# Forms written by ScalarE's queue, and branch blocks rounded where they lie, in a hybrid attention and convolution layer on one Trainium2 core

## The chip, the cores and the metric

The kernel runs on one core of a Trainium2 chip. The metric is the device time of one execution in microseconds. Three runs of the kernel before took 1036.29, 1038.19 and 1043.42 us; the median is 1038.19.

## The reference

One decoder layer for a sequence of 256 tokens with 2048 channels, all in float32. Cut to what matters here:

```python
h = _rmsnorm(x, pre_norm_g)
proj = jnp.einsum('bsd,de->bse', h, w_in)          # ten parts, see the split
(q_a, c_kv, k_rope, z_mla, c_in, b_gate, c_gate, z_conv, g_mla, g_conv) = jnp.split(proj, cuts, axis=-1)
...
q  = einsum(_rmsnorm(q_a), w_q_b)                   # 16 heads, 128 + 64 rotary
kv = einsum(_rmsnorm(c_kv), w_kv_b)                 # k_nope and v of 16 heads
attn = _causal_mla_attention(q_nope, q_rope, k_nope, k_rope, v)
attn = attn.reshape(b, s, MLA_WIDTH) * jax.nn.silu(z_mla)
y_mla = jnp.einsum('bse,ed->bsd', attn, w_o_mla)

u = c_gate * c_in
conv = sum(conv_w[k] * u_pad[:, k:k + s] for k in range(CONV_K))
y_conv = jnp.einsum('bse,ed->bsd', b_gate * conv * jax.nn.silu(z_conv), w_o_conv)

merged = jax.nn.sigmoid(g_mla) * y_mla + jax.nn.sigmoid(g_conv) * y_conv
x = x + _rmsnorm(jnp.einsum('bsd,de->bse', merged, w_out), post_norm_g)
```

All weights together are read once from DRAM, in units of 128 x 2048 float32 (1 MB).

## The kernel before

**Products.** A float32 value is split in a rounded part and the rest. `split_act` (L264) does it: ScalarE (ACT) rounds to `hi` (L265), VectorE (DVE) subtracts to `lo` (L266). A weight unit is loaded by SP's queue into `raw`, of which there are three slots (`load_raw`, L152), split in halves into `whi` and `wlo`, and multiplied on TensorE (PE), twice as many matmuls with `whi` as with `wlo`.

**Heads.** The first part loops over 16 heads. Around the attention of each head (queries `qn`, `qr`, keys `kn`, scores `sc` and `sw`, softmax `p`, its transposed `pt`, values `o`) it computes four units of the convolution path, `channels(h, 0)` to `channels(h, 3)`, whose sums `cv` are read by ACT (L811, L815, L818, tiles cv_f, cv_w, cg) or DVE before PE may overwrite them. Values are multiplied by their gate (L745) into `at_f`, four heads to a block: these four blocks are the attention's branch blocks. When the fourth head of a group is done, POOL's queue writes the block to DRAM (`far_at`, L749, 512 KB). The convolution's output goes by transposes and POOL writes to `far_cv` in the same way.

**Forms.** The gates g_mla and g_conv are products of x with two large weights. They are done as four sets s0 to s3 of seven products (Q1, V5, V6, V7, V3, V4, Q2) in place of eight, each with a combination of weights (DVE adds, L1272) and one of seven combinations of x, the "forms". `make_forms` (L876) prepares these while the heads run, a step at a time: three steps in each of the heads 0 to 13. It works in four chunks. For each, SP brings a part of x into `x_area` (256 KB twice), ACT scales it (L893), and then each of seven steps makes one form: ACT rounds (L907), DVE takes the rest (L909, L911), into one of three slots `form`. One step later the form's 256 KB are written to DRAM (`far_form`, L914), by SP's queue. ACT can round into a slot only when the write of the form three before has landed. The whole forms are read back by SP (`form`, L937) shortly before their product.

**Sets and branch blocks.** After the heads, the products of a set alternate with branch block products. p[0] to p[3] are the attention's (y_mla, sums `sq` with `at_both`), v[0] to v[3] the convolution's. Each has four weight units, one for each block, of 24 matmuls of 128x512 each (16 with `whi`, 8 with `wlo`); a named product of a set has 24 as well. `turned_unit` (above L969) loads a block from DRAM into a `raw` slot (`turned_at`, L969) and splits it into `at_both`. What follows on what is written by hand in calls of `interleave`; loads are then sorted by when their slot comes free and when they are needed, and issued up to 8 places ahead. For the first set:

```python
interleave(s0, {
    "Q1": p[0][:2], "V5": at_u[2:3] + p[0][2:3] + at_u[3:] + p[0][3:],
    "V6": p[1][:1], "V7": p[1][1:2], "V3": p[1][2:3], "Q2": p[1][3:] + p[2][:1],
})
```

Each engine and each of its DMA issues goes in the order of its own instructions: an instruction that waits holds back all that stand behind it on that engine. `tc.keep_in_program_order` fixes a place; the other instructions are moved by a scheduler.

Of the kernel before, what the change touches and what calls it, by code (L numbers as in the profile page):

```python
# [11 lines left out]
F32 = mybir.dt.float32  # L12
# [6 lines left out]
P = 128  # L19
S = 256  # L20
NT = S // P
# [61 lines left out]
def tile_layer(ctx: ExitStack, tc: tile.TileContext, xw, w0, xb, x, pos, pvec, post_g, wc, wz, wcv, wkr, wqk, wqr, wv, cwr, wsq, xf, out):  # L83
# [583 lines left out]
    def finish_all(*steps):  # L667
        for g in steps:
            for _ in g:
                pass  # L670
# [51 lines left out]
    def turn(p):  # L722

        pt = temp("pt", (P, 2, 3 * P), F32R, 1)
        hi, lo = (pt[:, j : j + 1, :].rearrange("p o (k q) -> p (o k) q", k=3) for j in range(2))
        split_act(quarters(hi), quarters(lo), by_rows(p[:, :], 3), True)
        return pt

    def values(h, pt):
        vv = groups["v", h // HV]  # L730
        j = h % HV
        o = bank(f"o{h}", tag="o", bufs=1)
        vs = slice(j * DV, (j + 1) * DV)
        both = o[:, :].rearrange("p (i q) -> p i q", i=2)
        mm = matmul
        mm(both, vv[0][:, 0, vs], pt[:, :, :S], start=True, stop=False)
        yield
        mm(o[:, :S], vv[1][:, 0, vs], pt[:, 0, :S], start=False, stop=False)
        mm(o[:, P:S], vv[1][:, 1, vs], pt[:, 0, S:], start=False, stop=False)
        mm(both[:, :, P:], vv[0][:, 1, vs], pt[:, :, S:], start=False, stop=True)  # L740

        at = at_t[:, h // HV, :, :].rearrange("p t (i k x) -> p t i k x", i=4, k=HV)[:, :, :, j, :]
        f = temp("f")
        whole(f[:, :], o)
        nc.vector.tensor_tensor(at, f[:, :].rearrange("p (t i x) -> p t i x", t=NT, i=4), at, op=ALU.mult)  # L745
        if j == HV - 1:
            g = h // HV
            tc.keep_in_program_order(
                nc.gpsimd.dma_start(out=far_at[g][:, :], in_=at_f[:, 4 * g : 4 * g + 4, :].rearrange("p k s -> p (k s)"))  # L749
            )  # L750


    at_t = at_f[:, :, :].rearrange("p (v t k) s -> p v t (k s)", v=NV, t=NT)
    far_at, far_cv, far_m = (
        [dram.tile([P, NT * 512], F32, name=f"far_{n}{g}") for g in range(4)] for n in ("at", "cv", "m")
    )
    z_ps = {}

# [31 lines left out]
    def channels(h, i):  # L790

        if i == 0:
            cv_ps["now"] = [bank(f"cv{h}_{t}", tag="cv", bufs=2) for t in range(NT)]
        quarter(cv_ps["now"], take(u_head[h][i]), i)
        if h == H - 2 and i in (0, 2):
            u = u_first[i // 2]
            tc.keep_in_program_order(nc.sync.dma_start(out=early[u][:, :], in_=plan[u][0]))
        if i == 3:
            if h == H - 1:
                at_u[0][0]()  # L800
                ahead(u_first[0])
                for u in at_u[:2]:
                    u[1](True)
            channels_done(*divmod(h, 4))

    def channels_done(j, n):
# [69 lines left out]
    def make_forms():  # L876

        kq = 2
        area = early_pool.tile([P, 2, kq, S], F32, name="x_area")
        sums_2 = [early_pool.tile([P, kq, P], F32, name=f"form_sum{i}") for i in range(2)]  # L880
        for c in range(KH // kq):
            for i in range(2):
                tc.keep_in_program_order(
                    nc.sync.dma_start(
                        out=area[:, i], in_=xf[i][:, c * kq * S : (c + 1) * kq * S].rearrange("p (k s) -> p k s", k=kq)
                    )
                )
            yield
            yield
            for i in range(2):  # L890
                for k in range(kq):
                    x = area[:, i, k, :]
                    nc.scalar.activation(x, x, AF.Copy, scale=col("pre_g", KH * i + kq * c + k))  # L893
            x = area[:, :, :, :].rearrange("p i k s -> p (i k) s")
            nc.vector.tensor_tensor(x, x, r_x[:, :].unsqueeze(1).to_broadcast([P, 2 * kq, S]), op=ALU.mult)
            yield
            a11, a21 = area[:, 0, :, :P], area[:, 0, :, P:]
            a12, a22 = area[:, 1, :, :P], area[:, 1, :, P:]
            u, w = (f[:, :, :] for f in sums_2)

            def tt(o, a, b, op):
                nc.vector.tensor_tensor(o, a, b, op=op)

            def part(n, src, sign=1.0):
                f = early_pool.tile([P, kq, 2, P], F32R, name=f"form{n}_{c}", tag="form", bufs=3)
                hi, lo = f[:, :, 0, :], f[:, :, 1, :]
                nc.scalar.activation(hi, src, AF.Copy, scale=sign)  # L907
                if sign == 1.0:
                    nc.vector.tensor_tensor(lo, src, hi.bitcast(F32), op=ALU.subtract)  # L909
                else:  # L910
                    nc.vector.scalar_tensor_tensor(lo, src, sign, hi.bitcast(F32), op0=ALU.mult, op1=ALU.subtract)  # L911
                w = kq * 2 * P
                return lambda: tc.keep_in_program_order(
                    nc.sync.dma_start(  # L914
                        out=far_form[n][:, c * w : (c + 1) * w], in_=f[:, :, :, :].rearrange("p k j c -> p (k j c)").bitcast(F32)
                    )
                )

            todo = (
                ("11", a11, 1.0, None), ("22", a22, 1.0, None), ("12", a12, 1.0, (u, a22, a21, ALU.subtract)),  # L920
                ("5", u, 1.0, (w, u, a11, ALU.add)), ("6", w, -1.0, (u, a11, a21, ALU.subtract)),
                ("7", u, 1.0, (w, w, a12, ALU.subtract)), ("3", w, 1.0, None),
            )
            for n, src, sign, following in todo:
                go = part(n, src, sign)
                if following:
                    tt(*following)
                yield
                go()
        while True:  # L930
            yield
# [64 lines left out]
            return list.__getitem__(self, i)  # L996

    at_b, cv_b = (Late(n, lambda i, n=n: both_tile(n, i)) for n in ("at", "cv"))
    at_u = [u for a, b in ((0, 2), (2, 3), (3, 4)) for u in turned_unit(far_at[a:b], at_b, a)]
    cv_u = [u for a, b in ((0, 2), (2, 4)) for u in turned_unit(far_cv[a:b], cv_b, a)]  # L1000
    for h in range(H):
        v, at = divmod(h, HV)
# [89 lines left out]
            rest = score(h + 1, later=True)  # L1092
        finish_all(*steps[::-1])
        if h == H - 1:
            pt = turn(ps_by_head.pop(h))
        channels(h, 3)
        if ahead_by_one:
# [4 lines left out]
        while len(coming) > ahead_by_one and h < H - 1:  # L1102
            arrive()
        if h == H - 1:
            finish_all(values(h, pt))
        if at == 3:
            coming.append(channels_join(v, 1))
        if at == 1 and h < H - 3:
# [251 lines left out]
    def interleave(s, after):  # L1360
# [12 lines left out]
    m_load = [turned_unit(far_m[a:b], m_b, a, tag, nc.gpsimd) for a, b, tag in ((0, 2, "rc0"), (2, 3, "rc1"), (3, 4, "rb1"))]  # L1373

    interleave(s0, {
        "Q1": p[0][:2], "V5": at_u[2:3] + p[0][2:3] + at_u[3:] + p[0][3:],
        "V6": p[1][:1], "V7": p[1][1:2], "V3": p[1][2:3], "Q2": p[1][3:] + p[2][:1],
    })
    interleave(s1, {"Q1": p[2][1:2], "V5": p[2][2:3], "V6": p[2][3:], "V7": p[3][:1], "V3": p[3][1:2], "V4": p[3][2:3], "Q2": p[3][3:]})
    interleave(s2, {  # L1380
# [288 lines left out]
```

## Time and profile before

| | |
|---|---|
| runs | 1036.29, 1038.19, 1043.42 us, median 1038.19 |
| profiled execution | 1039.11 us, of which the core's span 1037.3 |
| mean granted TensorE clock | 0.996 |
| busy: PE, DVE, ACT, POOL | 1011.0, 806.2, 591.8, 171.8 us |
| moved by DMA | 268.14 MB, 258 GB/s over the span |
| heads | to about 600 us of the span; sets and branch blocks follow |

Times of the trace are in microseconds from the start of the span. A row of a timeline has its start and length, the engine, the line, the operation, out<-in by the names of the tiles without their numbers, and how many instructions were grouped. Brackets give the idle time before it and what ended it. The rows of the waits give engine and line, what was waited for, and in total, times and longest. SPq, POOLq and ACTq are DMA issues of those engines.

### The profile page before, as it was taken

The page shows a single profiled execution, that of the slowest core. Times are in us where ns is not written, and L with a number is a line of the kernel's source. Part 1 is how long each engine was busy: PE and PEld are TensorE (multiplying, and loading weights), DVE is VectorE, ACT ScalarE, POOL GpSimd, SP SyncE. Part 2 cuts the span into 40 slices and gives each one's busy share as a digit, 9 for nine tenths or more (in the row PEclk, how much of TensorE's full clock was granted, in tenths as well). Part 3 has the DMA queues.
Part 4 walks back from the last instruction along what each step waited for, and adds up shares of the span by engine and source line. Part 5 has one row for each costly group of instructions (what it writes and reads, how often), then busy time and mean ns, then how long its engine had stood idle before and what let it go on. Part 6 is the DMA issues. An engine that isn't in the chain of part 4 may idle for free.

```text
span 1037.3 us, 13027 instructions
## 1 busy us (share of the span) xinstructions
PE 1011.0 (97%) x4552; PEld 836.9 (81%) x4552; DVE 806.2 (78%) x1103; ACT 591.8 (57%) x854; POOL 171.8 (17%) x315
## 2 busy tenths in 40 slices
PE   9999999999999999999999996999999999999997
PEld 8887888887888878778888875888788888878886
DVE  7589778767887677867787696889889779987562
ACT  7676656655665455555655463655665665565451
POOL 4520411203311222212133120000000101012000
PEclk9999999999999999999999998999999999999999
DMA  8775878668776688766688889697589979648842
GB/s 341 287 262 213 264 254 273 225 191 300 251 277 219 203 291 267 245 220 222 236 289 323 315 292 357 237 365 202 178 307 299 339 279 288 235 151 293 301 170 81
DMA packets 56674, 268.14 MB, mean 258 GB/s; under 512 B 9024, under 2 KB 13760, under 8 KB 31520
## 3 DMA queue, kind: packets, MB, share of 16 engines
q1 hardware_dynamic: 43488, 225.89, 59.9%
q0 software_dynamic: 12832, 40.23, 14.3%
q10 hardware_dynamic: 288, 1.20, 0.3%
q8 instruction: 35, 0.57, 0.2%
q14 instruction: 31, 0.25, 0.1%
HBM read 238.99 MB, written 24.12 MB: 254 GB/s over the span
## 4 chain that ended last, share of the span: by engine, by line
PE 88%; DMA 7%; DVE 3%; ACT 1%; issue 1%; SPq 0%; DVEq 0%; ACTq 0%
PE cv L88 28%; PE sq L88 16%; PE sX L88 8%; PE out L88 8%; PE z L88 8%; DMA far_form<-form 4%; PE sZ L88 4%; PE qa L88 2%; PE sY L88 2%; PE ckv L88 2%; PE vv L88 2%; PE kn L88 2%; PE qn L88 2%; DMA raw<-wsq_dram 1%; DVE wlo L266 1%; DMA x_area<-xf_dram 1%
## 5 line engine op out<-in xcount | busy, mean ns | idle before, releaser
L265 ACT ACTIVATE whi<-raw 128x1024 fp32r<-128x1024 f32 (+1 forms) x302 | 305.3, 1027 | 234.6 <-PE cv L88 89.4
L266 DVE TENSOR_TENSOR wlo<-raw,whi 128x1024 fp32r<-128x1024 f32 (+1 forms) x300 | 352.4, 1189 | 108.9 <-ACT whi L265 81.8
L88 PE MATMUL cv<-whi,x_both 128*128 128x512 f32 x1024 | 321.0, 390 | 4.7 <-ACT cv_f L811 2.9
L88 PEld LDWEIGHTS cv<-whi,x_both 128*128 128x128 f32 x1024 | 192.2, 188 | 46.1 <-ACT cv_f L811 3.7
L88 PE MATMUL cv<-wlo,x_both 128*128 128x512 f32 x512 | 199.6, 390 | 0.9 <-DVE wlo L266 0.9
L88 PEld LDWEIGHTS cv<-wlo,x_both 128*128 128x128 f32 x512 | 96.1, 188 | 20.3 <-DVE wlo L266 1.2
L266 DVE TENSOR_TENSOR slo_V<-b,shi_V 128x1024 fp32r<-128x1024 f32 x60 | 71.8, 1222 | 18.7 <-PE sq L88 12.1
L265 ACT ACTIVATE shi_V<-b 128x1024 fp32r<-128x1024 f32 x60 | 61.5, 1053 | 39.8 <-PE sq L88 22.7
L88 PE MATMUL z<-whi,x_both 128*128 128x512 f32 x256 | 79.9, 389 | 0.0
L366 POOL DMA_DIRECT2D far<-via x64 | 35.2, 557 | 227.1 <-DVE via L358 224.7
L88 PE MATMUL sq<-whi,at_both 128*128 128x512 f32 x256 | 63.4, 402 | 5.6 <-ACT whi L265 5.6
L88 PEld LDWEIGHTS sq<-whi,at_both 128*128 128x128 f32 x256 | 49.9, 195 | 16.7 <-ACT whi L265 6.0
L88 PE MATMUL sq<-whi,cv_both 128*128 128x512 f32 x256 | 60.6, 389 | 0.0
L88 PEld LDWEIGHTS sq<-whi,cv_both 128*128 128x128 f32 x256 | 48.0, 188 | 10.0
L88 PEld LDWEIGHTS z<-whi,x_both 128*128 128x128 f32 x256 | 48.1, 188 | 9.9
L88 PE MATMUL z<-wlo,x_both 128*128 128x512 f32 x128 | 49.8, 389 | 0.0
L88 PE MATMUL out<-whi,m_both 128*128 128x512 f32 x208 | 49.4, 389 | 0.0
L88 PE MATMUL sX<-shi_V,form 128*128 128x512 f32 x192 | 47.4, 389 | 0.0
L88 PEld LDWEIGHTS out<-whi,m_both 128*128 128x128 f32 x208 | 39.0, 188 | 8.1
L88 PEld LDWEIGHTS sX<-shi_V,form 128*128 128x128 f32 x192 | 36.0, 188 | 7.5
L1263 POOL DMA_DIRECT2D b<-wsq_dram x8 | 6.9, 863 | 208.6 <-DVE b L1272 95.7
L265 ACT ACTIVATE shi_Q<-b 128x1024 fp32r<-128x1024 f32 x28 | 28.8, 1052 | 22.1 <-PE sq L88 17.7
(305 smaller groups left out, 1572.7 us busy)
## 6 DMA issues: line engine op xcount, KB each, us to landing
raw<-wcv_dram SPq DMA_DIRECT2D x64, 1024.0 KB, 6.3
raw<-wsq_dram SPq DMA_DIRECT2D x48, 1024.0 KB, 6.9
b<-wsq_dram SPq DMA_DIRECT2D x26, 1024.0 KB, 5.1
raw<-wz_dram SPq DMA_DIRECT2D x16, 1024.0 KB, 4.9
raw<-wqk_dram SPq DMA_DIRECT2D x8, 1024.0 KB, 7.6
b<-wsq_dram POOLq DMA_DIRECT2D x8, 1024.0 KB, 9.2
far_form<-form SPq DMA_DIRECT2D x28, 256.0 KB, 7.5
form<-far_form SPq DMA_DIRECT2D x7, 1024.0 KB, 10.9
```

Of the source, the lines that this page charges most:

```text
L88: return tc.keep_in_program_order(nc.tensor.matmul(*a, **kw))
L265: a = nc.scalar.activation(hi, src, AF.Copy)
L266: b = nc.vector.tensor_tensor(lo, src, hi.bitcast(F32), op=ALU.subtract)
L366: tc.keep_in_program_order(queue.dma_start(out=f[i], in_=m))
L1263: tc.keep_in_program_order(nc.gpsimd.dma_start(out=dst[:, :], in_=wsq[n, c + b, k], accum_op=ALU.add))
```

## The change

Three things, in the words of the code. First, `far_form` is written by ACT's queue (`nc.scalar`) and not by SP's; the bringing of the next part of x moves one step ahead, to the last form of a chunk, and the first gets a step of its own. Second, the branch blocks no longer go to DRAM and back: `split_branch` rounds block i from `at_f` where it lies. Block 2 is rounded in the last head's `channels(15, 3)`, 0 and 1 before that head's `turn`, and 3 after its values; the first unit of p[0] is loaded and split ahead of those. Third, all four units of p[0] follow Q1, ahead of V5, and the units of p[1] move up or down to fit.

```diff
--- before.py
+++ after.py
@@ -743,16 +743,11 @@
         f = temp("f")
         whole(f[:, :], o)
         nc.vector.tensor_tensor(at, f[:, :].rearrange("p (t i x) -> p t i x", t=NT, i=4), at, op=ALU.mult)
-        if j == HV - 1:
-            g = h // HV
-            tc.keep_in_program_order(
-                nc.gpsimd.dma_start(out=far_at[g][:, :], in_=at_f[:, 4 * g : 4 * g + 4, :].rearrange("p k s -> p (k s)"))
-            )
 
 
     at_t = at_f[:, :, :].rearrange("p (v t k) s -> p v t (k s)", v=NV, t=NT)
-    far_at, far_cv, far_m = (
-        [dram.tile([P, NT * 512], F32, name=f"far_{n}{g}") for g in range(4)] for n in ("at", "cv", "m")
+    far_cv, far_m = (
+        [dram.tile([P, NT * 512], F32, name=f"far_{n}{g}") for g in range(4)] for n in ("cv", "m")
     )
     z_ps = {}
 
@@ -797,10 +792,8 @@
             tc.keep_in_program_order(nc.sync.dma_start(out=early[u][:, :], in_=plan[u][0]))
         if i == 3:
             if h == H - 1:
-                at_u[0][0]()
                 ahead(u_first[0])
-                for u in at_u[:2]:
-                    u[1](True)
+                split_branch(2)
             channels_done(*divmod(h, 4))
 
     def channels_done(j, n):
@@ -878,13 +871,17 @@
         kq = 2
         area = early_pool.tile([P, 2, kq, S], F32, name="x_area")
         sums_2 = [early_pool.tile([P, kq, P], F32, name=f"form_sum{i}") for i in range(2)]
-        for c in range(KH // kq):
+        def bring(c):
             for i in range(2):
                 tc.keep_in_program_order(
                     nc.sync.dma_start(
                         out=area[:, i], in_=xf[i][:, c * kq * S : (c + 1) * kq * S].rearrange("p (k s) -> p k s", k=kq)
                     )
                 )
+
+        bring(0)
+        yield
+        for c in range(KH // kq):
             yield
             yield
             for i in range(2):
@@ -911,7 +908,7 @@
                     nc.vector.scalar_tensor_tensor(lo, src, sign, hi.bitcast(F32), op0=ALU.mult, op1=ALU.subtract)
                 w = kq * 2 * P
                 return lambda: tc.keep_in_program_order(
-                    nc.sync.dma_start(
+                    nc.scalar.dma_start(
                         out=far_form[n][:, c * w : (c + 1) * w], in_=f[:, :, :, :].rearrange("p k j c -> p (k j c)").bitcast(F32)
                     )
                 )
@@ -925,6 +922,8 @@
                 go = part(n, src, sign)
                 if following:
                     tt(*following)
+                if n == "3" and c < KH // kq - 1:
+                    bring(c + 1)
                 yield
                 go()
         while True:
@@ -996,7 +995,11 @@
             return list.__getitem__(self, i)
 
     at_b, cv_b = (Late(n, lambda i, n=n: both_tile(n, i)) for n in ("at", "cv"))
-    at_u = [u for a, b in ((0, 2), (2, 3), (3, 4)) for u in turned_unit(far_at[a:b], at_b, a)]
+
+    def split_branch(i):
+        for t in range(NT):
+            split_turned(at_t[:, i, t, :], at_b[i], t, True)
+
     cv_u = [u for a, b in ((0, 2), (2, 4)) for u in turned_unit(far_cv[a:b], cv_b, a)]
     for h in range(H):
         v, at = divmod(h, HV)
@@ -1092,6 +1095,8 @@
             rest = score(h + 1, later=True)
         finish_all(*steps[::-1])
         if h == H - 1:
+            split_branch(0)
+            split_branch(1)
             pt = turn(ps_by_head.pop(h))
         channels(h, 3)
         if ahead_by_one:
@@ -1102,7 +1107,11 @@
         while len(coming) > ahead_by_one and h < H - 1:
             arrive()
         if h == H - 1:
+            load_raw(done["raw"])
+            split_unit(done["split"])
+            done.update(raw=done["raw"] + 1, split=done["split"] + 1)
             finish_all(values(h, pt))
+            split_branch(3)
         if at == 3:
             coming.append(channels_join(v, 1))
         if at == 1 and h < H - 3:
@@ -1373,8 +1382,7 @@
     m_load = [turned_unit(far_m[a:b], m_b, a, tag, nc.gpsimd) for a, b, tag in ((0, 2, "rc0"), (2, 3, "rc1"), (3, 4, "rb1"))]
 
     interleave(s0, {
-        "Q1": p[0][:2], "V5": at_u[2:3] + p[0][2:3] + at_u[3:] + p[0][3:],
-        "V6": p[1][:1], "V7": p[1][1:2], "V3": p[1][2:3], "Q2": p[1][3:] + p[2][:1],
+        "Q1": p[0], "V5": p[1][:1], "V6": p[1][1:2], "V7": p[1][2:3], "Q2": p[1][3:] + p[2][:1],
     })
     interleave(s1, {"Q1": p[2][1:2], "V5": p[2][2:3], "V6": p[2][3:], "V7": p[3][:1], "V3": p[3][1:2], "V4": p[3][2:3], "Q2": p[3][3:]})
     interleave(s2, {
```

Where the instructions go, at two places. The first is ACT at the end of head 8's channels, at the forms of the third chunk: form7_2 and form3_2 are forms 7 and 3 of that chunk, form3_2 takes the slot of form5_2 and so waits for its write; cv8 are the sums of head 8's channels, raw and whi are numbered by weight unit, qr, half, sc and sw belong to the next head's queries and scores. Before:

```order
L265 ACTIVATE whi76_0_3798<-raw76_3730 128x1024
L433 ACTIVATE half_3715<-qr5_3688 128x256
L907 ACTIVATE form3_2_3913<-form_sum1_1015 128x2x128
L811 ACTIVATE cv_f_110<-cv8_0_3547,r_both_97 128x512
L265 ACTIVATE whi76_1024_3802<-raw76_3730 128x1024
L265 ACTIVATE qr_3709<-f_3714 64x256 x2
L811 ACTIVATE cv_f_110<-cv8_1_3548,r_both_97 128x512
L695 ACTIVATE sc_half_3767<-sc9_3701 128x128
```

In the changed kernel, from the same cv_f on:

```order
L804 ACTIVATE cv_f_110<-cv8_1_3539,r_both_97 128x512
L695 ACTIVATE sc_half_3756<-sc9_3690 128x128
L695 ACTIVATE half_3757<-sw9_3691 128x256
L265 ACTIVATE whi77_0_3827<-raw77_3785 128x1024
L265 ACTIVATE qr_3698<-f_3703 64x256 x2
L904 ACTIVATE form7_2_3902<-form_sum0_1010 128x2x128
L265 ACTIVATE whi77_1024_3831<-raw77_3785 128x1024
L265 ACTIVATE pt_3859<-p_3458 128x384
L911 DMA far_form5_650<-form5_2_3820 128x512
L265 ACTIVATE whi78_0_3869<-raw78_3825 128x1024
L904 ACTIVATE form3_2_4108<-form_sum1_1011 128x2x128
L265 ACTIVATE whi78_1024_3873<-raw78_3825 128x1024
```

form3_2 stood ahead of both cv_f and now stands behind them, and the write that it waits for stands two rows ahead of it on the same queue, one whi apart.

The second place is SP's queue at the start of the first set. raw115 to raw118 are the weights of the four units of p[0], raw119 those of p[1]'s first; first_rb and first_rc are weights of the set's products, form_5, form_6 and form_7 the forms of V5, V6 and V7, turned_at2 and turned_at3 the blocks 2 and 3. Before:

```order
L167 DMA raw116_5798<-wsq_dram 128x2048
L1258 DMA first_rb0_5783<-wsq_dram 128x2048
L1258 DMA first_rb1_5784<-wsq_dram 128x2048
L937 DMA form_5_5782<-far_form5_654 128x2048
L969 DMA turned_at2_5803<-far_at2_642 128x1024
L1258 DMA first_rc0_5787<-wsq_dram 128x2048
L1258 DMA first_rc1_5788<-wsq_dram 128x2048
L167 DMA raw117_5828<-wsq_dram 128x2048
L969 DMA turned_at3_5852<-far_at3_643 128x1024
L937 DMA form_6_5789<-far_form6_655 128x2048
L167 DMA raw118_5943<-wsq_dram 128x2048
L937 DMA form_7_5790<-far_form7_656 128x2048
```

In the changed kernel:

```order
L167 DMA raw116_5805<-wsq_dram 128x2048
L167 DMA raw117_5807<-wsq_dram 128x2048
L1267 DMA first_rb0_5792<-wsq_dram 128x2048
L1267 DMA first_rb1_5793<-wsq_dram 128x2048
L936 DMA form_5_5791<-far_form5_650 128x2048
L1267 DMA first_rc0_5796<-wsq_dram 128x2048
L1267 DMA first_rc1_5797<-wsq_dram 128x2048
L167 DMA raw118_5827<-wsq_dram 128x2048
L936 DMA form_6_5798<-far_form6_651 128x2048
L167 DMA raw119_5852<-wsq_dram 128x2048
```

Both turned_at are gone, raw117 stands ahead of the set's first weights, raw118 ahead of form_6, and raw119 right behind form_6.

## Prediction

> **What bounds the kernel now.** I read the page first, for the engines and the transfers.
>
> ```profile
> PE 1011.0 (97%) x4552; PEld 836.9 (81%) x4552; DVE 806.2 (78%) x1103; ACT 591.8 (57%) x854; POOL 171.8 (17%) x315
> ```
>
> PE is busy for 1011.0 of 1037.3 us, so 26.3 us of idle time, with whatever is lost to a low clock, is all that a change which leaves the products alone can win. The change adds and removes no matmul. The next question is where those 26.3 us lie. PE's timeline at the end of the heads, where the products sX and sZ of the first set and the products sq of the branch blocks alternate, answers for the larger half (start, length, what ran, then the idle time before it and what ended that):
>
> ```profile
> 605.88 3.79 PE L88 MATMUL sq<-whi,at_both 128*128 128x512 f32 x16
> 611.16 0.73 PE L88 MATMUL sq<-wlo,at_both 128*128 128x512 f32 x2 [1.49 <-DVE wlo L266]
> 612.30 1.66 PE L88 MATMUL sq<-wlo,at_both 128*128 128x512 f32 x6 [0.41 <-DVE wlo L266]
> 613.79 3.79 PE L88 MATMUL sq<-whi,at_both 128*128 128x512 f32 x16
> ...
> 619.23 1.98 PE L88 MATMUL sZ<-shi_V,form 128*128 128x512 f32 x8
> ...
> 638.67 6.51 PE L88 MATMUL sq<-whi,at_both 128*128 128x512 f32 x16 [5.61 <-ACT whi L265]
> ...
> 646.84 1.98 PE L88 MATMUL sX<-shi_V,form 128*128 128x512 f32 x8
> ```
>
> The sixteen first matmuls of a unit take 3.79 us at 605.88 and 6.51 at 638.67, after a pause of 5.61 us: 2.7 more. The windows say why (length, busy time of PE, PEld, DVE, ACT and POOL, granted clock, DMA share, GB/s):
>
> ```profile
> 620.00:640.00 20.00, 12.22 (x49) 9.08 (x48) 13.90 (x14) 7.58 (x11) 0.89 (x1) 0.94 1.03 321
> 640.00:645.00 5.00, 5.00 (x14) 3.88 (x14) 4.42 (x4) 3.21 (x4) 0.00 (x0) 0.57 1.01 428
> ```
>
> The granted clock is 0.57 from 640 to 645, and the DMA engines are full in both windows. [...] What the pause waited for stands in SP's queue, the chain that ended last, and ACT's timeline, a row or a few of each:
>
> ```profile
> 612.27 0.33 SPq L167 DMA_DIRECT2D raw<-wsq_dram  x1
> 616.62 0.33 SPq L969 DMA_DIRECT2D turned_at<-far_at  x1
> 621.94 0.33 SPq L937 DMA_DIRECT2D form<-far_form  x1
> ...
> 624.69 12.76 DMA raw<-wsq_dram
> ...
> 637.56 2.00 ACT L265 ACTIVATE whi<-raw 128x1024 fp32r<-128x1024 f32 x2 [12.01 <-DMA raw<-wsq_dram]
> ```
>
> The weights of the last p0 unit were asked for at 624.69 and landed 12.76 us later; ACT stood for 12.01 us. Ahead of that issue on the queue are turned_at, which also holds a weight slot, and a form.
>
> The other losses that the change can touch lie earlier. First a row of the waits, ACT's, in all and how many times, then PE's stalls beside the making of the forms:
>
> ```profile
> ACT form L907 <- DMA far_form<-form: 30.5, 13, 6.1
> ...
> 141.87 0.39 PE L88 MATMUL sc<-kn,qn_hi 128*128 128x256 f32 x1 [0.54 <-DVE kn L266]
> 249.24 0.50 PE L88 MATMUL cv<-whi,x_both 128*128 128x512 f32 x1 [0.80 <-ACT cv_f L811]
> 386.07 0.50 PE L88 MATMUL cv<-whi,x_both 128*128 128x512 f32 x1 [2.10 <-ACT cv_f L811]
> 416.75 0.39 PE L88 MATMUL sc<-kn,qn_hi 128*128 128x256 f32 x1 [2.45 <-DVE kn L266]
> 447.17 0.50 PE L88 MATMUL cv<-whi,x_both 128*128 128x512 f32 x1 [1.77 <-ACT cv_w L815]
> ```
>
> ACT stood 13 times, 30.5 us in all, until a form's slot had been written away. The five stalls of PE sum to 0.54 + 0.80 + 2.10 + 2.45 + 1.77 = 7.66 us.
>
> **Branch blocks and their order.** Four writes far_at, four reads turned_at and their two weight slots go: 8 x 512 KB, 4 MB. The roundings of the blocks stay as many as before, on ACT and on DVE; they stand earlier. From 605.88 to 646.84 PE runs four units p0 and the product V5. A unit or a product is 24 matmuls, undisturbed from 613.79 to 619.23, 5.44 us. So 5 x 5.44 = 27.2 us of work took 40.96: 13.8 us lost.
>
> ```profile
> 604.22 3.89 ACT L265 ACTIVATE whi<-raw 128x1024 fp32r<-128x1024 f32 x4
> ...
> 620.95 1.14 ACT L265 ACTIVATE at_both<-turned_at 128x512 fp32r<-128x512 f32 x2
> ```
>
> What comes in its place, by hand from these rows: two roundings of a block on ACT, 1.14 us by the pair at 620.95, now stand ahead of the conv gate (cg) and of the weights' rounding at 604.22, and cg waits for a product on DVE that is itself behind a rounding. I let whi begin 2 us later. It was just in time (PE went on at 605.88 without a gap), so the first unit waits 2.0 us, and the 1.90 us for wlo that it stood before fall inside that: it ends at 605.9 + 2.0 + 5.4 = 613.3. The last p0 unit's weights need only the slot that the first unit's rounding frees near 612. At the 12.76 us of before they land at 624.8 and are rounded at 625.9, 1.7 us late, as that unit begins at 613.3 + 2 x 5.44 = 624.2; at the median of such loads, 6.9 us (below), they are 4 us early. I take no wait. Four p0 units and V5 then end at 613.3 + 4 x 5.44 = 635.1, 11.7 us earlier.
>
> Late next is p1's first unit, due at 635.1. Its weights stand on SP behind the form of V6, and that waits until POOL's writes far_cv have landed:
>
> ```profile
> 609.29 0.71 DVE L358 STREAM_TRANSPOSE cw<-cv_f 128x512 f32<-128x512 f32 x1
> ...
> 610.29 2.20 POOL L366 DMA_DIRECT2D far_cv<-cw  x4 [2.12 <-DVE cw L358]
> ...
> 616.85 0.55 POOL L366 DMA_DIRECT2D far_cv<-mv  x1 [2.74 <-DMA far_at<-at_f]
> ```
>
> The transpose falls behind roundings on DVE, to about 614; eight issues of 0.55 us reach 618.5, and the last landing came 5.1 us after its issue (616.85 to SP's next issue at 621.94), so SP is free near 623.5. At 12.76 us the weights land at 636.8 and are rounded at 637.9: a new wait of about 3 us. Bounds: none at 6.9 us; 6 us if the landing takes 16, and then, as before after 5.61, the half clock with its 2.7. I take 3, as the DMA engines stay near full. Net of these parts: 11.7 - 3.0 = **8.7 us**, bounds 3.0 and 11.7.
>
> **Forms by ACT's queue.** In the new order a form's write stands just ahead of the form that waits for its slot, in the typical place one whi of 1.06 us apart, some 25 times in 28. The wait on ACT is then about L - 1.1, where L is the write's time to landing. Rows of the form tiles, of the DMA issues (KB each, median us to landing) and of two windows:
>
> ```profile
> L914 SPq DMA_DIRECT2D far_form<-form x28: 327/427/784, 109.0 to 520.4; - x28
> ...
> DMA to landing us min/median/max: 3.8/7.7/14.8
> ...
> raw<-wsq_dram SPq DMA_DIRECT2D x48, 1024.0 KB, 6.9
> ...
> p<-far POOLq DMA_DIRECT2D x16, 192.0 KB, 4.8
> ...
> far_at<-at_f POOLq DMA_DIRECT2D x4, 512.0 KB, 5.9
> ...
> gb<-post_g_dram ACTq DMA_DIRECT2D x1, 1024.0 KB, 4.9
> ...
> 942.00:948.00 6.00, 6.00 (x28) 4.99 (x27) 6.00 (x10) 2.21 (x3) 2.54 (x5) 1.00 0.82 288
> 80.00:525.00 445.00, 436.47 (x2021) 363.09 (x2020) 347.27 (x587) 253.50 (x418) 89.67 (x164) 1.00 0.73 246
> ```
>
> The issues themselves, 28 x 0.43 = 12 us, go to an engine that is 57% busy; its lead over PE (next rows) hides them, and without that lead each would cost 0.43. On SP's queue 256 KB took a median of 7.7 us, among loads of 1 MB on the same queue. No write on ACT's queue is shown. Its one large transfer, 1 MB, issued at 942.9, landed in 4.9 us at a DMA share of 0.82, above the 0.73 of the forms' stretch; POOL's 192 KB took 4.8 and its writes of 512 KB 5.9. I take L = 4.7, nearest to ACT's own row; the bounds are 3.8, SP's fastest, and 7.7.
>
> How long ACT can stand unnoticed is in the trace too:
>
> ```profile
> 248.19 0.42 ACT L907 ACTIVATE form<-form_sum 128x256 fp32r<-128x256 f32 x1 [4.78 <-DMA far_form<-form]
> ...
> 385.03 0.42 ACT L907 ACTIVATE form<-form_sum 128x256 fp32r<-128x256 f32 x1 [6.08 <-DMA far_form<-form]
> ...
> 413.40 1.71 ACT L893 ACTIVATE x_area<-x_area,pv 128x256 f32<-128x256 f32 x4 [3.26 <-DMA x_area<-xf_dram]
> ```
>
> The first two waits stood ahead of cv_f and cost PE the 0.80 and 2.10 above; 4.78 - 0.80 and 6.08 - 2.10 are both 3.98 us of cover. At L = 4.7 a wait is 3.6, below it, so 0.54, 0.80, 2.10 and 1.77 go, 5.2 us. The 2.45 is not a form's: ACT stood 3.26 us for x_area, ahead of kn, and that load keeps its place on SP between the same weights, with one write less ahead of it; I let 0.8 go. Some of the 25 waits have less cover than 4 us; for those I take back 1.0. Net: **5.0 us**, bounds 6.5 (all but 1.2 of the 7.66) and a loss of 15.6 (first rival).
>
> **Sum.** 8.7 + 5.0 = 13.7 us off the profiled execution's 1039.11 is 1025.4. That execution lies 0.9 above the median of the runs, 1038.19; I say 1025.
>
> **Rivals.**
>
> ACT waits for its own writes (slower): if L is SP's 7.7 us, each wait is 6.6, 2.6 beyond the cover. Of 13 waits before, four stand beside a stall (0.54, 0.80, 2.10, 1.77); the same share of 25 is 8, so 8 x 2.6 = 20.8 us of stalls come and 5.2 go: 15.6 lost against 8.7 won, 1046. It decides from L = 5.1, and the kernel is slower than before from about L = 6.8. [...] The trace speaks against it as far as one transfer can, with 4.9 us for four times the bytes. Chance 0.10.
>
> The pause moves to p1: the wait of 6 us with half clock costs 8.7 where I took 3, 1031. For it: the landing of 12.76 us and the 321 GB/s (6.4 MB in 20 us), of which turned_at and far_at were 1 MB. Against: 12.76 was itself taken in the fullest stretch. 0.15.
>
> Forms gain nothing, L being near POOL's 5.9 so that 8 x 0.65 = 5.2 us of new stalls replace the old: 1030. 0.13.
>
> The change doesn't do what it says at the set's start: DVE, the engine behind the 1.49 and 0.41, gets its roundings in a burst and every unit waits for wlo; the 8.7 come back and 3 to 4 from the forms stay, 1036. 0.07.
>
> All waits go, p1's and x_area's too: 13.8 + 7.7 - 2.0 = 19.5 won, 1019.6. It is the near end of my forecast.
>
> **How the numbers follow.** The forecast, 1019 to 1029, has 0.55. The slower rival lies outside the range 1017 to 1037, the others inside; with the tails it leaves out some 0.15. A difference of 1%, 10.4 us, is about what a measurement of this kernel can tell from no change. Below 1027.8 lie nearly all of the forecast and some of the second and third rivals: 0.62. Above 1048.6 lies only the first rival with L over 8: 0.05. The rest, 0.33, is within 1%.
>
> **What would show it.** Right: far_form landing in about 4.7 us on ACT's queue; no stall of PE beside cv_f near 249 and 386; four p0 units in a row with one first wait of about 2 us, and no 12 us wait of ACT for raw; some 3 us of waiting at p1's first unit. Wrong: waits of ACT for far_form that average above 5 us, or a second stretch at half clock after V5.

## The result, and the profile after

The changed kernel took 1027.85 us in the median of four runs (1023.01, 1025.78, 1029.92, 1030.71) against 1038.60 for the kernel before on the same chip: a ratio of 0.989, 95% interval 0.9864 to 0.9916. Run again as an experiment it took 1026.72, ratio 0.9887 (0.9854 to 0.9919). The forecast was 1025. The first profiled execution took 1023.01 us with a span of 1021.2; the sum of the prediction for it was 1025.4.

Page of the changed kernel: the engines, then a group of its DMA issues (KB each, median us to landing) and two rows of its waits (total, times, longest).

```profile
PE 1006.6 (99%) x4552; PEld 835.5 (82%) x4552; DVE 805.2 (79%) x1103; ACT 591.4 (58%) x854; POOL 170.8 (17%) x311
...
far_form<-form ACTq DMA_DIRECT2D x28, 256.0 KB, 5.0
...
ACT form L904 <- DMA far_form<-form: 40.9, 14, 5.9
...
ACT whi L265 <- DMA raw<-wsq_dram: 10.9, 6, 3.6
```

PE's idle time fell from 26.3 to 14.6 us. The writes of the forms land in 5.0 us where they took 7.5, but ACT waits longer for them in all, 40.9 us against 30.5. Its wait for the set's weights fell from 18.7 us, 12.0 at the longest, to 10.9 and 3.6.

PE's timeline: the longest pause left in the heads, then from the first product of the set on:

```profile
411.89 0.39 PE L88 MATMUL sc<-kn,qn_hi 128*128 128x256 f32 x1 [1.97 <-DVE kn L266]
...
593.47 2.01 PE L88 MATMUL sX<-whi,form 128*128 128x512 f32 x8
...
601.08 3.98 PE L88 MATMUL sq<-whi,at_both 128*128 128x512 f32 x16 [1.97 <-ACT whi L265]
604.90 1.98 PE L88 MATMUL sq<-wlo,at_both 128*128 128x512 f32 x8
606.71 3.79 PE L88 MATMUL sq<-whi,at_both 128*128 128x512 f32 x16
...
617.59 3.79 PE L88 MATMUL sq<-whi,at_both 128*128 128x512 f32 x16
...
623.03 1.98 PE L88 MATMUL sZ<-shi_V,form 128*128 128x512 f32 x8
...
628.47 3.79 PE L88 MATMUL sq<-whi,at_both 128*128 128x512 f32 x16
...
683.76 1.98 PE L88 MATMUL sX<-shi_Q,form 128*128 128x512 f32 x8
```

Four p0 units and V5 run in a row, behind one wait of 1.97 us. p1's first unit follows at 628.47 without any. From 600 to 650 us the granted clock stays full, where before it was 0.57 in one window:

```profile
600.00:650.00 50.00, 48.92 (x215) 40.39 (x216) 44.83 (x40) 30.56 (x34) 6.19 (x10) 1.00 0.82 282
```

Why p1 does not wait is in the queues, POOL's and SP's issues and ACT's rounding of p1's weights:

```profile
609.67 2.18 POOL L366 DMA_DIRECT2D far_cv<-mv  x4
...
604.78 0.33 SPq L167 DMA_DIRECT2D raw<-wsq_dram  x1
613.42 0.33 SPq L936 DMA_DIRECT2D form<-far_form  x1
613.85 0.85 SPq L167 DMA_DIRECT2D raw<-wsq_dram  x2
...
624.73 2.01 ACT L265 ACTIVATE whi<-raw 128x1024 fp32r<-128x1024 f32 x2 [3.15 <-DMA raw<-wsq_dram]
```

The last p0 unit's weights are asked for at 604.78, ahead of everything that waits. SP comes free at 613.42, 2.1 us after POOL's last write was issued (the four writes in the first row start 0.55 us apart), and p1's weights land by 624.7, 10.9 us after their issue: rounded before 626.8, at least 1.7 us early.

Two distances hold all that changed much: from the start of the span to Q1 of the first set (the heads), and from there to Q1 of the second set, both read from PE's timelines. What follows took 336.1 us before and 336.5 to 337.5 us in the executions below.

| kernel (profiled execution) | heads | first set |
|---|---|---|
| before | 600.40 | 100.84 |
| the change, first profile | 593.47 | 90.29 |
| the change, second profile | 599.03 | 90.96 |
| forms by ACT's queue alone | 595.90 | 100.14 |
| branch blocks and order alone | 602.59 | 90.61 |
| the change, old order of p[0] | 597.83 | 100.35 |
| change, x by POOL's queue | 590.64 | 90.40 |
| change, forms by SP, x by POOL's queue | 596.90 | 90.95 |

The set is about 10 us shorter wherever the branch blocks and the order are both changed, and not with the order of before. The heads vary by 5.6 us between two executions of one kernel.

### The profile page after: what moved, and what is told of

It reads as the page before. It is cut to its first block, busy times and chain, and to the rows that moved or that the text cites. A ratio compares the mean times of both kernels' runs of the same rounds, so it can differ in the third digit from the quotient of the medians.

```text
span 1021.2 us, 13014 instructions
## 1 busy us (share of the span) xinstructions
PE 1006.6 (99%) x4552; PEld 835.5 (82%) x4552; DVE 805.2 (79%) x1103; ACT 591.4 (58%) x854; POOL 170.8 (17%) x311
## 4 chain that ended last, share of the span: by engine, by line
PE 85%; DMA 6%; ACT 3%; DVE 3%; issue 1%; POOL 1%; SPq 0%; DVEq 0%; ACTq 0%; POOLq 0%
PE cv L88 28%; PE sq L88 16%; PE out L88 9%; PE sX L88 7%; PE z L88 6%; PE sZ L88 4%; PE qa L88 2%; PE sY L88 2%; DMA x_area<-xf_dram 2%; PE ckv L88 2%; PE kn L88 2%; PE qn L88 2%; PE vv L88 2%; DMA far<-cw 1%; DMA b<-wsq_dram 1%
## 5 line engine op out<-in xcount | busy, mean ns | idle before, releaser
L88 PEld LDWEIGHTS cv<-whi,x_both 128*128 128x128 f32 x1024 | 192.3, 188 | 40.9 <-ACT cv_w L808 1.5
L265 ACT ACTIVATE shi_V<-b 128x1024 fp32r<-128x1024 f32 x60 | 61.6, 1054 | 40.9 <-PE sq L88 23.8
L88 PE MATMUL sq<-whi,at_both 128*128 128x512 f32 x256 | 60.8, 390 | 2.0 <-ACT whi L265 2.0
L265 ACT ACTIVATE shi_Q<-b 128x1024 fp32r<-128x1024 f32 x28 | 28.8, 1053 | 21.7 <-PE sq L88 19.1
```

Of the source, the lines that this page charges most:

```text
L88: return tc.keep_in_program_order(nc.tensor.matmul(*a, **kw))
L265: a = nc.scalar.activation(hi, src, AF.Copy)
```

## The experiments

**The change again.** Unaltered.

> The changed kernel once more, unaltered, for a second profiled execution and more times. In the first one the start of the first set came 6.9 us earlier than before, the set itself ended 10.5 us sooner beside that, and the profiled execution took 1023.0, while other executions of the same kernel took up to 1030.7 at a mean granted clock of 0.994 in place of 0.999. Theory: the slower executions have one more pause of TensorE of over 3 us, near the first unit of p1 or V5 at about 623 to 640 us, with a stretch at half clock behind it; then a profile of 1028 to 1031 shows it and one of 1023 does not. Rival: the difference is spread over the whole span (no pause, same clock in the trace).

1026.72 us (four runs, 1023.96 to 1028.66); the profiled execution took 1028.66. PE's timeline and the windows of that execution:

```profile
172.55 0.50 PE L88 MATMUL cv<-whi,x_both 128*128 128x512 f32 x1 [2.34 <-ACT cv_w L808]
...
310.06 0.50 PE L88 MATMUL cv<-whi,x_both 128*128 128x512 f32 x1 [1.41 <-ACT cv_w L808]
...
606.64 5.53 PE L88 MATMUL sq<-whi,at_both 128*128 128x512 f32 x16 [1.96 <-ACT whi L265]
```

```profile
174.00:176.00 2.00, 2.00 (x6) 1.52 (x6) 2.00 (x4) 2.00 (x5) 0.00 (x0) 0.50 0.20 80
...
608.00:610.00 2.00, 2.00 (x6) 1.57 (x5) 2.00 (x3) 2.00 (x4) 0.00 (x0) 0.50 0.00 0
```

The theory named the wrong place and the wrong length: there is no pause over 3 us and none at p1 or V5. The p0 pause is the same 1.96 us as in the first profile, but here a stretch at half clock followed it, and another followed the 2.34 us at 172.55; the sixteen matmuls took 5.53 us where they took 3.98. PE's idle time is 16.9 us where it was 14.6; these 2.3 us and the two stretches at half clock, 3.4 us long and worth 1.7 us each, make up the 5.65 us between the two executions.

**Part 1 alone.**

```diff
 # the kernel before, with make_forms of the change
-                    nc.sync.dma_start(out=far_form[n]...
+                    nc.scalar.dma_start(out=far_form[n]...
+                if n == "3" and c < KH // kq - 1:
+                    bring(c + 1)
```

> Part 1 alone: forms written by ACT's queue, the bringing of x a step earlier; branch blocks and order as before. Theory: far_form lands in about 5.0 us, the stalls of TensorE of 0.54, 0.80, 2.10 and 1.77 go, about 2 us stay at scores behind x_area; the set's start keeps its 12 us wait for raw. So 5 to 7 us faster than the kernel before, about 1032. Rival: the gain in the heads is given back at the set, since its weights are asked for no sooner: within 1 us of before.

1034.34 us against 1039.56, ratio 0.9949 (0.9921 to 0.9976): the theory. The four stalls are gone; two new ones of 1.16 and 0.97 us stand beside cv_w. The set's pause stands as before:

```profile
414.32 0.38 PE L88 MATMUL sc<-kn,qn_hi 128*128 128x256 f32 x1 [1.88 <-DVE kn L266]
...
634.25 5.73 PE L88 MATMUL sq<-whi,at_both 128*128 128x512 f32 x16 [5.23 <-ACT whi L265]
```

**Parts 2 and 3 alone.**

```diff
 # the changed kernel, with make_forms of before
-                    nc.scalar.dma_start(out=far_form[n]...
+                    nc.sync.dma_start(out=far_form[n]...
```

> Parts 2 and 3 alone: branch blocks rounded where they lie, four units of p0 ahead of V5; forms written by SP's queue as before. Theory: 10 to 11 us faster than before, about 1028, a first wait of 2 us at p0 and no wait of 12 us for raw; the form stalls of 7.7 us stay. Together with part 1 alone this adds up to the whole change (about 16 us in the profiled executions). Rival: the two parts overlap, and this alone gives as much as the whole change.

1028.15 us, ratio 0.991 (0.9877 to 0.9943): 9.4 us, the theory within its interval. With part 1's 5.3 that makes 14.7 us, against 11.8 for the whole change by the ratio in the same job; the intervals of some 3 us each do not exclude that they add up.

**The old order with the new blocks.**

```diff
-        "Q1": p[0], "V5": p[1][:1], "V6": p[1][1:2], "V7": p[1][2:3], "Q2": p[1][3:] + p[2][:1],
+        "Q1": p[0][:2], "V5": p[0][2:],
+        "V6": p[1][:1], "V7": p[1][1:2], "V3": p[1][2:3], "Q2": p[1][3:] + p[2][:1],
```

> The whole change but for the order: two units of p0 after Q1, the other two after V5, p1 as before. Theory: what counts is that the reads turned_at and their weight slots are gone, so that the weights are asked for earlier; the order is worth less than 2 us, and this gives 1026 to 1030. Rival: four units of p0 are what covers DVE's adding up of the weights for V5 (4.5 us of first_rt sums); with only two there, V5 waits 4 to 6 us for its weights, perhaps with half clock, and this is 5 us or more slower than the whole change.

1034.47 us, ratio 0.9952 (0.9928 to 0.9975): 6 to 8 us slower than the whole change. The theory fell, and the rival has the size but not the place: V5 did not wait. The time is that of part 1 alone (1034.34 us), and the first set took 100.35 us against 100.14 there: without the order, the new blocks won nothing. SP's queue, the chain that ended last, ACT's and PE's timelines:

```profile
617.76 0.33 SPq L936 DMA_DIRECT2D form<-far_form  x1
618.14 1.54 SPq L167 DMA_DIRECT2D raw<-wsq_dram  x2
...
618.14 16.53 DMA raw<-wsq_dram
...
634.77 2.00 ACT L265 ACTIVATE whi<-raw 128x1024 fp32r<-128x1024 f32 x2 [12.56 <-DMA raw<-wsq_dram]
...
635.88 6.22 PE L88 MATMUL sq<-whi,at_both 128*128 128x512 f32 x16 [6.41 <-ACT whi L265]
```

Two p0 units and V5 cover less time than four units and V5. The last p0 unit's weights stand behind the form that waits for POOL's writes, take 16.53 us, and PE stops for 6.41 us. So the old pause of 5.61 us comes back in full without any turned_at: that the weight slots are free is not enough, the order has to change too. The new order with the old blocks was not run.

**Forms by SP's queue, x a step earlier.**

```diff
-                    nc.scalar.dma_start(out=far_form[n]...
+                    nc.sync.dma_start(out=far_form[n]...
```

> The whole change but for the queue: forms written by SP's queue again, with x brought a step earlier as in the change, branch blocks and order as in the change. Theory: it is the queue that wins the heads (a landing of 5 us in place of 7.5, and no place behind weight loads), and the earlier bringing of x is worth nothing; so this is as branch blocks alone, 1028 to 1030, with the start of the first set near 607 as there, 5 us later than in the whole change. Rival: the earlier bringing of x, by which later steps of the forms are free sooner, is what wins; then this is as the whole change, 1025 to 1028.

1032.56 us, ratio 0.9916 (0.9884 to 0.9948), against 0.991 with x at its old step too: with the forms on SP's queue, bringing x earlier wins nothing. The whole change is 3 us faster by the ratios (0.9887) and 5 to 6 by the medians; the intervals of the ratios overlap. The pause at scores was 3.92 us in its profile, and behind x_area again:

```profile
417.04 0.58 PE L88 MATMUL sc<-kn,qn_hi 128*128 128x256 f32 x1 [3.92 <-DVE kn L266]
...
413.09 0.91 ACT L890 ACTIVATE x_area<-x_area,pv 128x256 f32<-128x256 f32 x2 [4.14 <-DMA x_area<-xf_dram]
```

**Block 2 rounded later.**

```diff
                 ahead(u_first[0])
-                split_branch(2)
 ...
+            split_branch(2)
             finish_all(values(h, pt))
```

> The whole change with block 2 rounded later: behind the first p0 unit's weights and no longer ahead of the second conv gate of the last head. Theory: the 1.97 us wait of TensorE at the first p0 unit is the chain block 2's rounding, DVE's product, cg, rounding of the weights; without the first link the wait falls to under 1 us, and with it goes the half clock that followed it in one of two executions (1.5 to 2 us): 1 to 4 us faster than the whole change, 1023 to 1026. Rival: DVE is late there anyway (weights' rest, conv gate), and the wait stays at 1.5 to 2 us with the time of the whole change.

1025.33 us, ratio 0.9855 (0.9804 to 0.9907), not to be told from the whole change. PE's timeline:

```profile
172.21 0.50 PE L88 MATMUL cv<-whi,x_both 128*128 128x512 f32 x1 [2.79 <-ACT cv_w L807]
...
605.06 3.97 PE L88 MATMUL sq<-whi,at_both 128*128 128x512 f32 x16 [1.09 <-ACT whi L265]
```

The pause at p0 fell from 1.97 to 1.09 us, and no half clock followed it: block 2's rounding made a little under half of that pause. What is won there is less than the pauses in the heads, here one of 2.79 us, differ between executions.

**x brought by POOL's queue.**

```diff
-                    nc.sync.dma_start(
+                    nc.gpsimd.dma_start(
                         out=area[:, i], in_=xf[i][:, c * kq * S : ...
```

> The whole change with x brought for the forms by POOL's queue in place of SP's. Theory: the wait of TensorE at scores (1.97 and 1.26 us in two executions at about 412 to 417) is ACT's wait for x_area, whose load stands behind a weight load of 1 MB on SP's queue; on POOL's queue it lands earlier and that wait goes: 1 to 2 us faster than the whole change, and the smaller wait for cv_w near 170 goes with it if it has the same cause. Rival: POOL's queue is held by its own waits for DVE (transposes of the softmax), so the load is issued later and the waits grow: 2 us or more slower.

1019.88 us (1019.31 to 1021.20), ratio 0.9801 (0.976 to 0.9842): more than was expected, and clear of the change's own interval. Windows of its heads:

```profile
100.00:200.00 100.00, 100.00 (x471) 83.93 (x470) 79.08 (x137) 62.91 (x108) 21.28 (x39) 1.00 0.76 263
200.00:300.00 100.00, 100.00 (x466) 83.60 (x465) 78.83 (x131) 52.24 (x83) 26.60 (x49) 1.00 0.76 254
300.00:400.00 100.00, 100.00 (x461) 83.55 (x460) 77.39 (x129) 59.01 (x96) 19.18 (x36) 1.00 0.70 233
400.00:500.00 100.00, 100.00 (x469) 83.75 (x468) 79.65 (x135) 58.91 (x100) 18.17 (x34) 1.00 0.70 238
```

PE is never idle for 400 us. But the reason given was only half right. x was the cause at both places of the theory: near 170 too ACT stood for x_area right ahead of that cv_w, 1.67 to 3.89 us in the five profiles with x on SP's queue and the forms written once on ACT's, and PE's pause was 1.1 us less each time (0.58 to 2.79). The first row is of the second profile of the change. But on POOL's queue the last part of x is not early; it is issued later than before, and ACT's scaling of it has moved with it:

```profile
171.42 0.51 ACT L890 ACTIVATE x_area<-x_area,pv 128x256 f32<-128x256 f32 x1 [3.44 <-DMA x_area<-xf_dram]
...
424.00 1.10 POOL L877 DMA_DIRECT2D x_area<-xf_dram  x2 [0.27 <-issue]
...
429.83 0.90 ACT L890 ACTIVATE x_area<-x_area,pv 128x256 f32<-128x256 f32 x2
```

In the changed kernel this last part was asked for at 401 and scaled at 408.5, ahead of kn, whose products PE waits for. Here it is scaled at 429.8, with no wait, ahead of a cv_w that is not urgent. What moved is a place in ACT's order; how much of it is the queue and how much the place was not separated. The forms tell the same. Their writes land in 6.1 us here, the slowest of all profiles with ACT's queue where each is written once, and ACT stands up to 6.59 us for a slot, without any stall of PE:

```profile
372.37 0.42 ACT L904 ACTIVATE form<-form_sum 128x256 fp32r<-128x256 f32 x1 [6.59 <-DMA far_form<-form]
```

**Every form written twice.**

```diff
-                return lambda: tc.keep_in_program_order(nc.scalar.dma_start(out=far_form[n]...
+                def go():
+                    for far in (far_spare, far_form[n]):
+                        tc.keep_in_program_order(nc.scalar.dma_start(out=far...
+                return go
```

> The whole change with every form written twice by ACT's queue, first to a spare place and then to its own: 7 MB more, so that the wait is for the second of two writes. A test of the slower rival of the prediction, in which the landing time L decides. Theory: the landing time seen by the waiting form grows from 5.0 to 6 to 7 us; by the prediction's price (a cover of 4 us, waits of L less 1.1, about 8 places) that is 8 x 1 to 2 = 7 to 15 us more than the whole change; with the 14 waits that the trace of the change really shows in place of 25, half of that, 4 to 8 us: 1031 to 1035. Rival: ACT has far more lead than 4 us at most places, and this costs under 2 us.

1036.77 us, ratio 0.9973 (0.9943 to 1.0003): some 9 us of the change's gain are gone, more than the 4 to 8 us of the theory and within the 7 to 15 us of the prediction's price. Its waits, and PE's timeline:

```profile
ACT form L905 <- DMA far_form<-form: 58.2, 20, 9.6
...
416.10 0.58 PE L88 MATMUL sc<-kn,qn_hi 128*128 128x256 f32 x1 [4.59 <-DVE kn L266]
...
526.32 0.50 PE L88 MATMUL cv<-whi,x_both 128*128 128x512 f32 x1 [1.70 <-ACT cv_f L804]
...
532.28 0.50 PE L88 MATMUL cv<-whi,x_both 128*128 128x512 f32 x1 [2.91 <-ACT cv_f L804]
```

ACT's waits grew from 40.9 to 58.2 us in all, 9.6 at the longest, and stalls beside cv_f are back, so longer waits can cost what the slower rival says. But the largest pause, 4.59 us with half clock for 6.8 us behind it, stands behind x_area, for which ACT stood 2.13 us, as in the change. How much of the 9 us is the forms' waiting, and how much the 7 MB more for the other transfers, was not separated.

**Forms by SP's queue, x by POOL's.**

> The whole change with x brought by POOL's queue and the forms written by SP's queue again: the two queues apart. Theory: x on POOL's queue wins 5 to 7 us by itself (in the whole change with x on POOL's queue no pause of TensorE was left in the heads), and the forms' queue matters little once x is early, since the waits of ACT for forms were no shorter in all on its own queue (40.9 us against 30.5): 1020 to 1024. Rival: the forms' writes on SP's queue, behind weight loads, still stop ACT ahead of cv_f, cv_w and kn: the heads keep 4 us or more of pauses, 1025 to 1030.

1025.67 us, ratio 0.9875 (0.984 to 0.9911): the rival. With x out of the way the forms' queue still decides 6 to 8 us (0.9801 with ACT's, and 1019.69 us in the next run). Pauses of 1.75 and 2.71 us at scores were left, the second behind a form on ACT, 2.49 us late, and kn behind that:

```profile
276.92 0.42 ACT L904 ACTIVATE form<-form_sum 128x256 fp32r<-128x256 f32 x1 [2.49 <-DMA far_form<-form]
```

**x by POOL's queue, p0's weights rounded ahead of the conv gates.**

```diff
                 ahead(u_first[0])
-                split_branch(2)
+                load_raw(done["raw"])
+                split_unit(done["split"])
+                done.update(raw=done["raw"] + 1, split=done["split"] + 1)
 ...
-            load_raw(done["raw"]) ... split_unit(done["split"]) ...
+            split_branch(2)
             finish_all(values(h, pt))
```

> The whole change with x brought by POOL's queue, the first p0 unit's weights rounded in the last head's channels, ahead of its conv gates, and block 2 after that. Theory: the wait of 1.96 us at the first p0 unit, which is the last of its size, goes or falls under 1 us, and with it the half clock of 3.4 us that followed it in 4 of 7 executions: 2 to 3 us faster than with x on POOL's queue alone (1019.9), 1016 to 1018, with executions within 2 us of each other. Rival: the weights' rest, now ahead of the conv gate on DVE, delays the conv blocks (far_cv) and with them the form of V6 and p1's weights, which gives the 2 us back there: 1019 to 1021.

1019.69 us (six runs, 1019.25 to 1020.46), ratio 0.9814 (0.9784 to 0.9844): the same as with x by POOL's queue alone. PE's timeline:

```profile
595.48 3.79 PE L88 MATMUL sq<-whi,at_both 128*128 128x512 f32 x16
...
605.00 0.73 PE L88 MATMUL sq<-wlo,at_both 128*128 128x512 f32 x2 [0.28 <-DVE wlo L266]
...
652.99 2.12 PE L88 MATMUL sZ<-shi_V,form 128*128 128x512 f32 x8 [1.68 <-DVE sc L1319]
```

The pause at p0 is gone (0.28 and 0.40 are left) and p1's first unit starts 1.05 us sooner, counted from Q1, but V3 waits 1.68 us for DVE where it waited 0.68: the gain is given back there, 29 us later, and not at p1 as the rival had it. The first set took 90.34 us against 90.40.

## Why the prediction was right

**The bound and the places.** PE's idle time and its half clock were all there was to win. The two stretches named, the forms in the heads and the set's start, are where it came from. (Two readings were off without weight in the sum: the blocks held three weight slots and not two, as blocks 0 and 1 shared one, and 7.7 us was the median of the 28 writes and the seven readings back; the writes alone took 7.5.)

**The set's start** was forecast at 8.7 us and came to 10.6 (100.84 to 90.29; 9.4 by the runs of that part alone). Its first two terms hold: the first p0 unit waits 1.97 us for 2.0, by the chain forecast, rounding of block 2, product on DVE, cg, whi; p1's first unit is due 35.0 us after Q1's start, forecast 34.7. The third, 3 us of waiting at p1, did not come. It was mis-sized in two steps. POOL's last write landed in 2.1 us and not in 5.1, so that SP came free 20.0 us after Q1's start and not 23.1; the DMA share was 0.52 around these writes (604 to 613.8), and 1.01 before (612 to 624). And the weights landed in 10.9 us, not 12.76. That the blocks' reads and writes are gone doesn't explain the second: the old order lacks them too, and there the weights behind the same form took 16.53 us and cost 6.41; in the changed kernel itself the slowest of the two loads asked for next took 21.7 us. So the step was sound: here the load had 14.6 us until PE came to p1 (613.85 to 628.47), and in the old order the like load had 11.3.

**The forms** were forecast at 5.0 us. Part 1 alone gave 5.3 by its ratio; the heads of the profiles gave 6.9, 4.5 and 1.4 us. L was 5.0 for the 4.7 assumed, so ACT's own large transfer was nearer than SP's median; over all profiles the medians are 5.0 to 6.1 us on ACT's queue and 7.2 to 8.0 on SP's, with each form written once. But the mechanism was only half right, and that its size came out is in part luck. The forecast had 25 waits of 3.6 us, each within a cover of 4 us. There were 14, of 2.9 us on average and up to 5.9, more in all than before. And 4 us was the cover of two places only: at the stall of 1.77 us ACT had stood 2.83, a cover of 1.06, so that a wait of 3.6 there would have cost more than before. The stalls went because the forms no longer stand there. The first row is of the kernel before, the others are the changed kernel's second cv_f of head 8 with form7_2 and form3_2, of which form3_2 had stood ahead of it:

```profile
445.25 0.42 ACT L907 ACTIVATE form<-form_sum 128x256 fp32r<-128x256 f32 x1 [2.83 <-DMA far_form<-form]
...
382.04 0.69 ACT L804 ACTIVATE cv_f<-cv,r_both 128x512 f32<-128x512 f32 x1 [0.30 <-PE cv L88]
387.32 0.42 ACT L904 ACTIVATE form<-form_sum 128x256 fp32r<-128x256 f32 x1 [2.40 <-DMA far_form<-form]
394.33 0.42 ACT L904 ACTIVATE form<-form_sum 128x256 fp32r<-128x256 f32 x1 [4.28 <-DMA far_form<-form]
```

PE lost less because the waits stand at other places. In the four profiles with the forms on SP's queue, four to six forms that waited for their slot stand one or two instructions ahead of a cv_f, cv_w or kn; in the eight with ACT's queue, none. Two of the four differ from a kernel of the eight by the queue alone, so the scheduler moved the forms with it: queue and place changed together, and no run moved one alone. The pause behind x_area was forecast to keep 1.65 of its 2.45 us and kept 1.97, 1.26 and 1.88. New pauses were allowed 1.0 us; beside cv_w they were 0.58 us in one execution, 3.75 in the other and 2.13 with part 1 alone, and the one near 170 in each is x's, whose earlier bringing was given no price.

**The sum** was 13.7 us. The first profile shows 16.1, the medians 10.75 and 12.8. What the sum lacks is a term for pauses that differ from execution to execution, and for the half clock behind the short ones, which the prediction gave only to pauses of more than 5 us. The first profile had no such stretch, the second two.

**The rivals.** The slower one did not come, though by its own rule it should have: it decides from L = 5.1, and with x by POOL's queue L was 6.1, some 8 us of stalls by its price, where the heads had none. Longer waits can still cost, as writing each form twice suggests. That the pause moves to p1, and that the set's start gains nothing, did not happen.

## What to carry to other kernels

Before a transfer is given another queue, look at the instruction that stands right behind the wait: here ACT's waits grew in all, and PE stood less, as the forms had come to stand behind the readers of PSUM and not ahead of them. A stall that a trace blames on a transfer may need more than one thing to go: with the slots free and the old order it stayed whole. Change such things one at a time. A time to landing held for its place alone: weights of 1 MB at the start of the set took 10.9, 12.76 and 16.53 us in three orders.

## What the hardware showed that was not expected

Short pauses of PE brought the half clock in some executions and not in others. The wait at p0's first unit was 1.96 or 1.97 us in eight profiles; behind five of them the granted clock was at half for 3.4 us, behind three not at all. Lost time at half clock, by the granted clock of the windows after each pause, in all eleven profiles and that of before, without the pause ahead of the last product, where the program ends:

| pause of PE | pauses | followed by half clock |
|---|---|---|
| 0.86 to 1.77 us | 24 | none |
| 1.88 to 2.96 us | 20 | 11, of 3.4 us each |
| 3.92 to 6.41 us | 5 | 5, of 6.8 us or more |

Three of 1.70 to 1.77 us are left out, as a longer pause followed within 9 us; behind one of them, with part 1 alone, the clock was at half 1.2 us before the longer pause began. The stretches came in steps of 3.4 us, each worth 1.7 us of matmuls.

Where a pause fell decided most of it. In each of the twelve profiles the granted clock changed only at times that lie whole steps of 3.413 us apart, over the whole span: in that of before the half clock lasted 6.83 us, two steps, and the next change came 392.53 us after its end, 115 steps. Cut PE's timeline at these steps, from 90 to 1005 us, and take those that began at full clock. All 14 with 1.96 us or more of idle time were followed by a step at half clock, two of the five with 1.71 to 1.93 us, and none with 1.6 us or less. The wait at p0 lay within one step in the five profiles where half clock followed; in the other three a border cut it, and the larger part was 1.19, 1.56 or 1.57 us. Here are two steps of the second profile of the change, then two with x by POOL's queue (length, busy time of PE, PEld, DVE, ACT and POOL, granted clock, DMA share, GB/s):

```profile
603.46:606.87 3.41, 1.45 (x7) 0.91 (x6) 3.41 (x8) 1.92 (x3) 0.00 (x0) 1.00 0.71 298
606.87:610.29 3.41, 3.41 (x9) 2.64 (x9) 3.41 (x5) 3.41 (x5) 0.00 (x0) 0.50 0.01 2
...
593.64:597.05 3.41, 2.64 (x12) 1.87 (x10) 3.41 (x6) 1.62 (x4) 0.00 (x0) 1.00 1.00 420
597.05:600.46 3.41, 2.23 (x10) 1.74 (x11) 3.41 (x6) 3.41 (x6) 0.00 (x0) 1.00 0.16 67
```

The first step has 1.96 us without work, and the next is at half clock; the same pause cut in 0.77 and 1.19 us left the clock full. Where the steps lay differed between executions, so one such pause spreads the times of a kernel by an estimated 1.7 us. With x by POOL's queue, where one is left, the runs lie within 1.9 us of each other.
